# State products in four bands of PSUM rows, with a buffer of its own for the convolution gate, in a hybrid recurrent trunk on one core

## The chip, the cores and the metric

The kernel runs on one core of a Trainium2 chip. The metric is the device time of one execution in microseconds; the kernel before has a median of 1597.33 us over three runs (1597.06 to 1597.72). Engine names are those of the profile: PE is the matrix engine (PEld its weight loads), DVE the vector engine, ACT the activation engine, POOL the general one, SP issues the DMAs.

## The reference

One step of a one-layer trunk over 1072 tokens: 16 meta tokens, 1024 prompt tokens, and 8 samples of 4 tokens each. All of them share the weights; each sample starts from its own saved states.

```python
x = rmsnorm(h, norm_w)
z = x @ w_in                      # gates, and the inputs of four branches, 512 wide each
# A: GLA, 4 heads, key width 64     S_t = diag(exp g_t) S_{t-1} + k_t^T v_t ;  o_t = q_t S_t
# B: HGRN2, 4 heads, key width 128  the same recurrence with k = 1 - f
# C: mLSTM, 4 heads                 stabilised matrix memory
# D: conv module                    GLU -> causal depthwise conv, width 31 -> LayerNorm -> swish
y_b = W_b(silu(zgate_b) * mixer_b)
h = h + (sum_b sigmoid(gate_b) * y_b) @ w_out ;  out = rmsnorm(h, final_norm)
```

The outputs are the two token groups without the meta tokens, and the new states of the prompt and of each sample.

## The kernel before

All values are float32. A projection splits its weights and its activations into a high and a low part and adds three products for each block of 128 input features: in `mm3` these are L185, L186 and L187, in `pair` L277, L278 and L279. One projection of 128 output columns takes 24 matmuls for each group of about 356 tokens. `split_w` makes the two weight parts: the high one on ACT (L138), the low one on POOL, or on DVE where `E=V` is given (L139).

The program runs in stages, and each engine takes its instructions in one fixed order. That order is made before the run by a scheduler that simulates the program; it may move an instruction ahead of others whose operands it thinks will come later. `tc.cur_priority` pushes work back in that choice: the 31-tap convolution adds 700 to it.

1. **Entry (to about 100 us).** The 1072 token rows are read in nine tiles h0 to h8, normalised, transposed (L174) in three groups of three tiles, and evacuated as `xh` (ACT, L178) and `xl` (DVE, L179). One raw gate weight is loaded behind the first three tiles and split on DVE. A few gates (`gate_direct`) and the small projections (`small`) follow; `combine_x` makes the operand sums of the next stage.
2. **Pairs (about 90 to 500 us).** `pair` computes two projections of 128 columns at once by a Strassen-like scheme: seven half-size products instead of eight, each over 4 feature blocks and two token slices (s = 0, 1) of 268 columns. Its PSUM tiles are `sa` (tag a, two buffers, one for each slice) and `sb`, `sc`, `sd` (tag r, five buffers). There are 19 pairs: four `conv_pair` and fifteen `pair_to`. Each `conv_pair` is followed by the 31-tap convolution on DVE (`conv_taps`: one L386 and 30 L388 over 1024 columns), which reads its tile `u`; `u` has one buffer, and the next `conv_pair` writes its sigmoid into it (L349, ACT, straight from `sa`) before it multiplies it there (L352, DVE).
3. **Recurrences (about 500 to 1290 us).** Four HGRN2 units, two GLA units and four mLSTM units, with projections between them (`filler` adds gates). A recurrent unit projects f, k, q and v; `vtok` transposes v into token rows (`tta`, three PSUM tiles from `acc_tile`, which has three buffers in all, then `v9p` from the same ones); `levels` builds the intra-chunk attention in halving levels (`lv`, L636, after which DVE scales q and k in place, L651 and L652, before the next level may read them); `linear_unit` forms the chunk states and the outputs (`op`).
   In `linear_unit` the last chunk holds 16 prompt tokens and the 32 sample tokens, 48 rows (`TAIL`). Each sample's rows meet another state, so nine products go into one PSUM region: for each of them `qblk` holds a stationary block, zero but for the columns of that sample (48 columns wide in HGRN2, 112 in GLA, where two heads lie at rows 0 and 64). The attention inside the chunk is added by L816 (once or twice 48 rows). GLA also has diagonal sums `dg` (L760): nine products with 128 stationary columns and two moving ones.
4. **Branches and output (about 1290 us to the end).** Four branch projections, the gated sum and the output projection.

Of the kernel before, what the change touches and what calls it, by code (L numbers as in the profile page):

```python
# [65 lines left out]
def trunk(ctx, tc, hx, w_in, w_sm, w_br, w_out, pk, wgk2, mlb, fnorm, s_gla, s_hg, s_c, s_n, s_m, s_cv,  # L66
# [82 lines left out]
    with tc.tile_pool(name="x0", bufs=9, side="right", reuse_waits="tile") as x0:  # L149
        hs = []  # L150
# [7 lines left out]
        for i0 in (0, 3, 6):  # L158
# [9 lines left out]
            if i0 == 0:  # L168
                raw0 = load_raw(w_in, OFF["gate"])
# [10 lines left out]
            if i0 == 0:  # L180
                w0 = split_w(raw0, E=V)
# [70 lines left out]
    def pair(c0, c1, c11, c12, c22, c21):  # L252
# [20 lines left out]
        def prod(w, o, x, s, out, start, stop):  # L273
            xa, xb = (t[:, :, s * HS:(s + 1) * HS] for t in xs[x])
# [19 lines left out]
        for s in range(2):  # L294
            prod(w1, KH, "a12", s, a[s], False, True)
            c11(s, a[s])
# [7 lines left out]
        for s in range(2):  # L304
            prod(w4, 0, "s4", s, c[s], False, True)
            V.tensor_tensor(h(p1, s), h(u2, s), c[s], ALU.add)
# [6 lines left out]
    def pair_to(sec, i, dst, func, times=False, base=0):  # L313
# [27 lines left out]
        pair(o, o + P, c11, rest(i + 1, False), rest(i + 1, True), rest(i, True))  # L341

    def conv_pair(i):
        u = gtl("u", [P, UW + NSEQ * 34])
        us = u[:, UW:].rearrange("p (s x) -> p s x", x=34)
        G.memset(u[:, 0:30], 0.0)

        def c11(s, ps):
            S.activation(u[:, 30 + s * HS:30 + (s + 1) * HS], ps, AF.Sigmoid)  # L349

        def c12(t):
            V.tensor_tensor(u[:, 30:30 + HT], t, u[:, 30:30 + HT], ALU.mult)  # L352
# [88 lines left out]
    gate_direct(0, w=w0)  # L441
    gate_direct(1)
# [73 lines left out]
    qblk2 = mx.tile([P, (NSEQ + 1) * WT], F32, name="qblk", tag="qblk")  # L516
    G.memset(qblk2, 0.0)
    qblkb = [qblk2[:, 0:480], qblk2[:, 480:960]]
    cnt = {"att": 0}
# [10 lines left out]
    def csz(c):  # L530
        return min(P, NT - c * P)
# [43 lines left out]
    def vtok(sec, i, ones_col=False):  # L575
# [12 lines left out]
        v9 = split3(x9, 1, "v9", 4, acc_tile("v9p"))  # L588
# [109 lines left out]
    def qblk_both(qv):  # L698

        for i in range(2):  # L700
            r = slice(64 * i, 64 * i + 64)
            c = WT + 64 * i + NM
            for s in range(NSEQ):
                e = c + s * (WT + NDEC)
                G.tensor_copy(qblk2[r, e:e + NDEC], qv[r, i, NP + s * NDEC:NP + (s + 1) * NDEC])
            G.tensor_copy(qblk2[r, 64 * i:64 * i + NM], qv[r, i, NPR:NP])
        return lambda s: qblk2[:, s * WT:(s + 1) * WT]
# [8 lines left out]
    def z_out(o, rstd, nw, gate, zi, mu=None):  # L716
# [4 lines left out]
        else:  # L721
# [15 lines left out]
    def rms(os, epss):  # L737
# [4 lines left out]
        for i, o in enumerate(os):  # L742
# [3 lines left out]
            S.activation(sq[:TAIL, 8], o[:TAIL, 8], AF.Square, accum_out=ms[:TAIL, 9 * i + 8:9 * i + 9])  # L746
# [7 lines left out]
    def linear_unit(uid, qv, nh, k, f, prod, vts, s0, epss, finish, pout, sout):  # L754
        rw = P // nh
        if nh == 2:
            ps = mmt("dg")
            for c in range(9):
                n = csz(c)
                T.matmul(ps[:n, 2 * c:2 * c + 2], prod[:, c * P:c * P + n], onesb, start=True, stop=True)  # L760
# [49 lines left out]
        qb = qblk_both(qv) if nh == 2 else qblk_for(qv[:, 0], uid % 2)  # L810
        w = WT if nh == 2 else TAIL
        for s in range(1, NSEQ + 2):
            s %= NSEQ + 1
            T.matmul(ps[:w], qb(s), s0[:, s - 1] if s else sall[:, 7], start=(s == 1), stop=False)
# [532 lines left out]
```

## Time and profile before

| what | value |
|---|---|
| median of three runs | 1597.33 us |
| profiled execution, its own time | 1597.18 us |
| span of its trace | 1595.4 us |
| mean granted PE clock | 0.989 |
| DMA | 176.40 MB, mean 111 GB/s |
| DVE, ACT, POOL busy | 65%, 35%, 30% of the span |

The span leaves out 1.8 us of the execution's time. Averages say little here, since the four stages have different limits; the views of a window show each of them by itself. "Idle before, releaser" means how long an engine stood still before an instruction, and whose end let it go on. A matmul of float32 that is not a transpose or one of the split products shows as two instructions in the trace, since the array passes over it twice.

### The profile page before, as it was taken

What the parts mean: (1) busy time and instruction counts of PE and PEld (TensorE: products, weight loads), DVE (VectorE), ACT (ScalarE), POOL (GpSimd) and SP (SyncE); (2) the same over time, 40 slices, a digit from 0 to 9 for tenths busy, and PEclk for the clock granted to TensorE, in tenths of its full rate; (3) what the DMA queues carried; (4) which work ended last, traced back from release to release, by engine and by line L of the source; (5) the groups of instructions that cost most, each with busy time, mean ns of one, the idle gap of its engine ahead of it and who ended that gap; (6) DMA issues with size and microseconds to landing.
All of it is one profiled execution on the core that took longest, in us unless ns stands there. A gap on an engine that the chain in (4) does not pass through costs nothing.

```text
span 1595.4 us, 30033 instructions
## 1 busy us (share of the span) xinstructions
PE 1558.2 (98%) x12366; PEld 1496.5 (94%) x12366; DVE 1035.6 (65%) x1827; ACT 554.0 (35%) x1095; POOL 470.9 (30%) x418
## 2 busy tenths in 40 slices
PE   7999999899999999999999999999999999999998
PEld 6999999899999899999998998999999999999886
DVE  7959979999996446444544565476665646744533
ACT  6534343243433333323424323323323244422211
POOL 2222322123223232223232323222322313877300
PEclk9999999999999999999999999999999999999999
DMA  5423233231337113131323132144323277676231
GB/s 190 133 80 101 92 91 107 88 108 51 110 100 236 42 48 104 56 100 56 104 60 94 55 97 82 49 148 135 117 72 88 89 248 224 179 236 208 80 111 54
DMA packets 190572, 176.40 MB, mean 111 GB/s; under 512 B 9260, under 2 KB 164800, under 8 KB 190436
## 3 DMA queue, kind: packets, MB, share of 16 engines
q1 hardware_dynamic: 190436, 174.49, 35.6%
q8 instruction: 97, 1.59, 0.4%
q14 instruction: 39, 0.32, 0.1%
HBM read 122.45 MB, written 52.00 MB: 109 GB/s over the span
## 4 chain that ended last, share of the span: by engine, by line
PE 78%; DVE 16%; issue 3%; DMA 2%; ACT 1%; SPq 0%; DVEq 0%; POOLq 0%; ACTq 0%
PE acc L187 18%; PE acc L185 18%; PE acc L186 18%; DVE y L388 7%; PE lv L636 2%; DVE wl L139 2%; PE sa L277 1%; PE sa L278 1%; PE sa L279 1%; PE sc L278 1%; PE sc L277 1%; PE sc L279 1%; PE sd L279 1%; PE op L800 1%; PE sd L278 1%
## 5 line engine op out<-in xcount | busy, mean ns | idle before, releaser
L139 POOL TENSOR_TENSOR wl<-wraw,wh 128x1024 fp32r<-128x1024 f32 (+1 forms) x124 | 272.2, 2196 | 632.7 <-ACT wh L138 628.0
L185 PE MATMUL acc<-xh,wh 128*128 128x352 f32 (+2 forms) x1320 | 437.5, 332 | 2.1 <-ACT vt L539 1.2
L187 PE MATMUL acc<-xh,wl 128*128 128x352 f32 (+2 forms) x1320 | 436.7, 331 | 0.0
L186 PE MATMUL acc<-xl,wh 128*128 128x352 f32 (+2 forms) x1320 | 435.5, 330 | 0.0
L185 PEld LDWEIGHTS acc<-xh,wh 128*128 128x128 f32 x1320 | 251.7, 191 | 5.6 <-ACT vt L539 1.9
L187 PEld LDWEIGHTS acc<-xh,wl 128*128 128x128 f32 x1320 | 251.0, 190 | 3.2 <-issue 0.9
L186 PEld LDWEIGHTS acc<-xl,wh 128*128 128x128 f32 x1320 | 251.4, 190 | 1.8 <-issue 0.7
L388 DVE SCALAR_TENSOR_TENSOR y<-u,pkt,y 128x1024 f32<-128x1024 f32 x120 | 191.2, 1593 | 0.7
L138 ACT ACTIVATE wh<-wraw 128x512 fp32r<-128x512 f32 (+1 forms) x125 | 110.4, 883 | 231.0 <-PE acc L186 135.8
L185 PE MATMUL acc<-zh,wh 128*128 128x352 f32 x384 | 124.5, 324 | 0.0
L186 PE MATMUL acc<-zl,wh 128*128 128x352 f32 x384 | 124.3, 324 | 0.0
L187 PE MATMUL acc<-zh,wl 128*128 128x352 f32 x384 | 124.2, 324 | 0.0
L277 PE MATMUL sa<-xh,wh 128*128 128x268 f32 x304 | 88.7, 292 | 6.6 <-ACT u L349 6.3
L278 PE MATMUL sa<-xl,wh 128*128 128x268 f32 x304 | 88.2, 290 | 0.0
L279 PE MATMUL sa<-xh,wl 128*128 128x268 f32 x304 | 87.8, 290 | 0.0
L651 DVE TENSOR_TENSOR q<-q,tot 128x256 f32<-128x256 f32 (+3 forms) x96 | 46.4, 483 | 54.5 <-PE lv L636 53.7
L1179 POOL TENSOR_TENSOR mix<-mix,gt 128x352 f32<-128x352 f32 x72 | 73.1, 1030 | 28.9 <-DVE gt L1178 25.7
L185 PEld LDWEIGHTS acc<-zh,wh 128*128 128x128 f32 x384 | 72.2, 188 | 0.4 <-DVE gt L1178 0.4
L187 PEld LDWEIGHTS acc<-zh,wl 128*128 128x128 f32 x384 | 72.3, 188 | 0.0
L186 PEld LDWEIGHTS acc<-zl,wh 128*128 128x128 f32 x384 | 72.2, 188 | 0.0
L277 PEld LDWEIGHTS sa<-xh,wh 128*128 128x128 f32 x304 | 58.3, 192 | 7.3 <-ACT u L349 6.8
L1178 DVE TENSOR_TENSOR gt<-acc,gt 128x352 f32<-128x352 f32 x72 | 36.2, 518 | 39.5 <-PE acc L187 36.6
(393 smaller groups left out, 3367.3 us busy)
## 6 DMA issues: line engine op xcount, KB each, us to landing
wraw<-w_in SPq DMA_DIRECT2D x92, 512.0 KB, 3.9
gt<-gscr SPq DMA_DIRECT2D x30, 528.0 KB, 4.7
gscr<-gd SPq DMA_DIRECT2D x60, 176.0 KB, 1.8
zr<-zscr SPq DMA_DIRECT2D x16, 528.0 KB
wraw<-w_br SPq DMA_DIRECT2D x32, 256.0 KB, 2.9
gt<-sscr SPq DMA_DIRECT2D x12, 528.0 KB, 4.1
zscr<-gt SPq DMA_DIRECT2D x12, 528.0 KB, 2.6
sscr<-u SPq DMA_DIRECT2D x16, 268.0 KB, 2.3
```

The lines of the kernel that those rows point to most:

```text
L138: S.activation(hi[:, :kd], raw[:, :kd], AF.Copy)
L139: (E or G).tensor_tensor(lo[:, :kd], raw[:, :kd], hi[:, :kd], ALU.subtract)
L185: T.matmul(ps, wh(k), ah(k), start=(i == 0), stop=False)
L186: T.matmul(ps, wh(k), al(k), start=False, stop=False)
L187: T.matmul(ps, wl(k), ah(k), start=False, stop=(i == kd - 1))
L277: T.matmul(out, wh, xa[:, k], start=start and k == 0, stop=False, skip_group_check=True)
L278: T.matmul(out, wh, xb[:, k], start=False, stop=False, skip_group_check=True)
L279: T.matmul(out, wl, xa[:, k], start=False, stop=stop and k == KH - 1, skip_group_check=True)
L388: V.scalar_tensor_tensor(ymain, u[:, NM + j:NM + j + NPR], w(j), ymain, ALU.mult, ALU.add)
L651: V.tensor_tensor(qx[:, :, 1], qx[:, :, 1], pv[r, :, 0:1].broadcast_to([rw, nb, h]), ALU.mult)
L1178: V.tensor_tensor(gt[:, t0:t0 + n], ps[:, :n], gt[:, t0:t0 + n], ALU.mult)
L1179: G.tensor_tensor(mixed[j][:, t0:t0 + n], mixed[j][:, t0:t0 + n], gt[:, t0:t0 + n], ALU.add)
```

## The change

Seven edits, all in one kernel:

- **Last chunk in bands.** The 48 rows of the last chunk are spread over 128 PSUM rows. Two samples share a band of 32 rows, so a state product has 32 stationary columns (`qblk_bands`) and goes into one of four bands, in the order of samples 0, 2, 4, 6, 1, 3, 5, 7, then the prompt state (once for each head in GLA). The attention block is spread the same way into a new tile `attp` (48 x 128) by two ACT copies in HGRN2 and by two DVE operations for each head in GLA; these also take over the diagonal term, which a POOL multiply did before. The outputs, their mean squares and the last transposes then run over 128 rows, and `z_out` gathers the 48 columns again with two DVE operations in place of one.
- **Diagonal sums in bands.** Each of the nine `dg` products becomes up to four of 32 stationary columns, 34 for a GLA unit.
- **Fewer copies for `qblk`.** In GLA 6 POOL copies instead of 18, in HGRN2 3 instead of 2.
- **Convolution gate.** `conv_pair` writes its sigmoid into a tile of the tag `g11` (two buffers) instead of `u`.
- **Meta tokens.** In the fifteen `pair_to`, the products a12 and s4 leave out the 16 meta columns in the first slice: 252 columns instead of 268.
- **Entry.** Two gate weights are loaded behind the first three token tiles, and both are split on DVE, in the middle of the first group's transposes, instead of one there and one on POOL.
- **PSUM and tiles.** `v9p` takes a buffer of `mmt` instead of `acc_tile`; two small tiles share the buffer of another tag.

```diff
...
             if i0 == 0:
-                raw0 = load_raw(w_in, OFF["gate"])
+                raws = [load_raw(w_in, OFF["gate"] + j * P) for j in range(2)]
             for k in range(KD):
...
+                if i0 == 0 and k in (1, 5):
+                    wg01.append(split_w(raws[k // 4], E=V))
...
-        def prod(w, o, x, s, out, start, stop):
-            xa, xb = (t[:, :, s * HS:(s + 1) * HS] for t in xs[x])
+        def prod(w, o, x, s, out, start, stop, m=0):
+            m = m if s == 0 else 0
+            out = out[:, m:]
+            xa, xb = (t[:, :, s * HS + m:(s + 1) * HS] for t in xs[x])
...
-            prod(w1, KH, "a12", s, a[s], False, True)
+            prod(w1, KH, "a12", s, a[s], False, True, m)
...
         def c11(s, ps):
-            S.activation(u[:, 30 + s * HS:30 + (s + 1) * HS], ps, AF.Sigmoid)
+            S.activation(g11[:, s * HS:(s + 1) * HS], ps, AF.Sigmoid)
 
         def c12(t):
-            V.tensor_tensor(u[:, 30:30 + HT], t, u[:, 30:30 + HT], ALU.mult)
+            V.tensor_tensor(u[:, 30:30 + HT], t, g11, ALU.mult)
...
-        v9 = split3(x9, 1, "v9", 4, acc_tile("v9p"))
+        v9 = split3(x9, 1, "v9", 4, mmt("v9p"))
...
+    def spread(t, i):
+        return (t[:, 32 * i:32 * i + 32].rearrange("p (c x) -> p c x", x=16)[:, :, 8:16],
+                t.rearrange("p (s x) -> p s x", x=16)[:, :, 4 * i:4 * i + NDEC])
+
+    def dense(t):
+        return t[:, 0:NM].rearrange("p (c x) -> p c x", x=8), t[:, NM:TAIL].rearrange("p (s j) -> p s j", j=NDEC)
+
+    def qblk_bands(qv, nh, buf):
+        qb = qblk2[:, buf * 320:buf * 320 + 320]
+        for i in range(nh):
+            r = slice(i * (P // nh), (i + 1) * (P // nh))
+            q = qv[r, i, NPR:NT]
+            d = qb[r, 0:256].rearrange("p (b w) -> p b w", w=64)
+            sm = q[:, NM:].rearrange("p (b a j) -> p a b j", a=2, j=NDEC)
+            for a in range(2):
+                e = 48 * a + 4 * i
+                G.tensor_copy(d[:, :, e:e + NDEC], sm[:, a])
+            G.tensor_copy(spread(qb[r, 256:320], i)[0], dense(q)[0])
+        return lambda s: qb[:, 32 * s:32 * s + 32]
...
-                T.matmul(ps[:n, 2 * c:2 * c + 2], prod[:, c * P:c * P + n], onesb, start=True, stop=True)
+                for b in range(0, n, 32):
+                    e = min(b + 32, n)
+                    T.matmul(ps[b:e, 2 * c:2 * c + 2], prod[:, c * P + b:c * P + e], onesb, start=True, stop=True,
+                             skip_group_check=True)
...
-        w = WT if nh == 2 else TAIL
-        for s in range(1, NSEQ + 2):
-            s %= NSEQ + 1
-            T.matmul(ps[:w], qb(s), s0[:, s - 1] if s else sall[:, 7], start=(s == 1), stop=False)
+        for a in (0, 2, 4, 6, 1, 3, 5, 7, 8, 9)[:NSEQ + nh]:
+            b = 32 * (a // 2 if a < NSEQ else a - NSEQ)
+            T.matmul(ps[b:b + 32], qb(a), s0[:, a] if a < NSEQ else sall[:, 7], start=(a in (0, 2, 4, 6)), stop=False,
+                     skip_group_check=True)
         for hi_, ((vt, _), (_, att8)) in enumerate(zip(vts, atts)):
-            T.matmul(ps[64 * hi_:64 * hi_ + TAIL], att8, vt[:TAIL, 8, 0:P], start=False, stop=True)
+            for d, x, e in zip(spread(attp[hi_], hi_), dense(att8), dense(ident[:TAIL, :TAIL])):
+                if nh == 2:
+                    V.scalar_tensor_tensor(d, e, dgv[:TAIL, 8, hi_:hi_ + 1], x, ALU.mult, ALU.add)
+                else:
+                    S.activation(d, x, AF.Copy)
+            T.matmul(ps, attp[hi_], vt[:TAIL, 8, 0:P], start=False, stop=(hi_ == nh - 1), skip_group_check=True)
+        for o in outs:
+            S.activation(o[:, 8], ps, AF.Copy)
```

How the order moves on PE, at three places. A number behind a name tells tiles of one name apart; it differs by a few between the two kernels. The first place is the pair that follows the third `conv_pair`. Before, its `sb` came straight after the last products of the `conv_pair` (`sd_3012`):

```order
L279 MATMUL sd_3012<-xh_96,wl_2890 128x268
L277 MATMUL sd_3012<-xh_96,wh_2889 128x268
L278 MATMUL sd_3012<-xl_97,wh_2889 128x268
L279 MATMUL sd_3012<-xh_96,wl_2890 128x268
L277 MATMUL sb_3126<-sh_824,wh_3109 128x268
L278 MATMUL sb_3126<-sl_825,wh_3109 128x268
```

and its first `sa` some hundred matmuls later, behind its own `sc` and `sd`:

```order
L277 MATMUL sd_3239<-xh_96,wh_3116 128x268
L278 MATMUL sd_3239<-xl_97,wh_3116 128x268
L279 MATMUL sd_3239<-xh_96,wl_3117 128x268
L277 MATMUL sa_3124<-xh_96,wh_3102 128x268
L278 MATMUL sa_3124<-xl_97,wh_3102 128x268
L279 MATMUL sa_3124<-xh_96,wl_3103 128x268
```

In the changed kernel `sa` stands at the same place as in the program, ahead of `sb`:

```order
L282 MATMUL sd_3015<-xh_96,wl_2893 128x268
L280 MATMUL sd_3015<-xh_96,wh_2892 128x268
L281 MATMUL sd_3015<-xl_97,wh_2892 128x268
L282 MATMUL sd_3015<-xh_96,wl_2893 128x268
L280 MATMUL sa_3127<-xh_96,wh_3105 128x268
L281 MATMUL sa_3127<-xl_97,wh_3105 128x268
L282 MATMUL sa_3127<-xh_96,wl_3106 128x268
```

So `sa` moved ahead by about a hundred matmuls, and nothing but the two `sa` buffers of the `conv_pair` stands between them. The second place is the first GLA unit on PE, at the end of its second `vtok`. Before, the levels' products (`lv`) stood between the transposes (`tta`), and the next level followed at once:

```order
L538 MATMUL tta_9501<-ident_70,vf_9412 128x128 x2
L636 MATMUL lv_9595<-q_9114,k_9125 32x32 x3
L538 MATMUL tta_9501<-ident_70,vf_9412 128x128 x2
L538 MATMUL tta_9507<-ident_70,vf_9412 128x128
L636 MATMUL lv_9595<-q_9114,k_9125 32x32 x29
L640 MATMUL lvt_9631<-q_9114,k_9125 48x48
L538 MATMUL tta_9507<-ident_70,vf_9412 128x128 x3
L538 MATMUL tta_9513<-ident_70,vf_9412 48x128
L557 MATMUL v9p_9516<-ident_70,x9_9414 96x128
L636 MATMUL lv_9640<-q_9114,k_9125 32x32 x16
```

In the changed kernel the transposes stand together, the diagonal sums come behind them, and a projection follows:

```order
L547 MATMUL tta_9525<-ident_70,vf_9436 128x128 x4
L547 MATMUL tta_9531<-ident_70,vf_9436 128x128 x4
L547 MATMUL tta_9537<-ident_70,vf_9436 48x128
L566 MATMUL v9p_9540<-ident_70,x9_9438 96x128
L788 MATMUL dg_9551<-onesb_77,prod_9234 32x2 x33
L788 MATMUL dg_9551<-onesb_77,prod_9234 16x2
L649 MATMUL lvt_9635<-q_9138,k_9149 48x48
L185 MATMUL acc_9886<-xh_96,wh_9882 128x352
L186 MATMUL acc_9886<-xl_97,wh_9882 128x352
```

There each later level of this unit has 24 projection matmuls between itself and the level before it. The third place is the last chunk of the first HGRN2 unit, on PE; before:

```order
L802 MATMUL op<-sall,q 128x128
L814 MATMUL op<-s_5922,qblk 48x128 x8
L814 MATMUL op<-sall,qblk 48x128
L816 MATMUL op<-vt,att_5617 48x128
L187 MATMUL acc<-xh,wl 128x356
```

and in the changed kernel:

```order
L830 MATMUL op<-sall,q 128x128
L841 MATMUL op<-s_5930,qblk 32x128 x8
L841 MATMUL op<-sall,qblk 32x128
L849 MATMUL op<-vt,attp_5625 128x128
L186 MATMUL acc<-xl,wh 128x356
```

The neighbours are the same; the nine state products write 32 rows each, and the one that closes them writes all 128.

More of the change, by code (lines that the diff above doesn't have):

```diff
@@ L149, in trunk @@
     with tc.tile_pool(name="x0", bufs=9, side="right", reuse_waits="tile") as x0:
-        hs = []
+        hs, wg01 = [], []
         def load_h(i):
@@ L250, in combine_x, with pair @@
                   s3=(sh[:, 1], sl[:, 1]), s4=(sh[:, 2], sl[:, 2]))
-    def pair(c0, c1, c11, c12, c22, c21):
+    def pair(c0, c1, c11, c12, c22, c21, m=0):
         wp = pools["gph"]
@@ L304, in pair @@
         for s in range(2):
-            prod(w4, 0, "s4", s, c[s], False, True)
+            prod(w4, 0, "s4", s, c[s], False, True, m)
             V.tensor_tensor(h(p1, s), h(u2, s), c[s], ALU.add)
@@ L339, in rest @@
             return ev
-        pair(o, o + P, c11, rest(i + 1, False), rest(i + 1, True), rest(i, True))
+        pair(o, o + P, c11, rest(i + 1, False), rest(i + 1, True), rest(i, True), NM)
     def conv_pair(i):
         u = gtl("u", [P, UW + NSEQ * 34])
+        g11 = stt("g11")
         us = u[:, UW:].rearrange("p (s x) -> p s x", x=34)
@@ L440, in trunk @@
     open_pool("gph", bufs=1)
-    gate_direct(0, w=w0)
-    gate_direct(1)
+    for j in range(2):
+        gate_direct(j, w=wg01[j])
     small()
@@ L515, in trunk @@
     WT = 64 + TAIL
-    qblk2 = mx.tile([P, (NSEQ + 1) * WT], F32, name="qblk", tag="qblk")
+    qblk2 = mx.tile([P, 960], F32, name="qblk", tag="qblk")
     G.memset(qblk2, 0.0)
     qblkb = [qblk2[:, 0:480], qblk2[:, 480:960]]
+    attp = []
+    for i in range(2):
+        t = mx.tile([TAIL, P], F32, name=f"attp{i}", tag=f"attp{i}")
+        G.memset(t, 0.0)
+        attp.append(t)
     cnt = {"att": 0}
@@ L696, in qblk_for @@
         return lambda s: qb[:, s * TAIL:(s + 1) * TAIL]
[L698 to L707, printed above, removed]
+    def spread(t, i):
[15 more added lines that the diff above has]
+        return lambda s: qb[:, 32 * s:32 * s + 32]
     def vblk_for(v9, s0, s1):
@@ L714, in vblk_for, with z_out @@
         return vb
-    def z_out(o, rstd, nw, gate, zi, mu=None):
+    def z_out(o, rstd, nw, gate, zi, mu=None, head=0):
         if mu is not None:
@@ L724, in z_out @@
                                 ALU.mult)
-            V.tensor_scalar(o[:TAIL, 8], o[:TAIL, 8], rstd[:TAIL, 8:9], None, ALU.mult)
+            V.tensor_scalar(o[:, 8], o[:, 8], rstd[:, 8:9], None, ALU.mult)
         for c0, c1 in QUADS:
-            n = csz(c0)
+            bands = c0 == 8 and mu is None
+            n = P if bands else csz(c0)
             ps = mmt("zt")
@@ L730, in z_out @@
                 T.transpose(ps[:, (c - c0) * P:(c - c0) * P + n], o[:n, c, :], ident[:n, :n])
+            if bands:
+                for x, g in zip(spread(ps[:, :P], head), dense(gate[:, NPR - NM:])):
+                    V.scalar_tensor_tensor(g, x, nw, g, ALU.mult, ALU.mult)
+                continue
             a = NM if c0 == 0 else 0
@@ L964, in ml_n0 @@
     def ml_n0():
-        r = tl("n0", [32, P], 1)
+        r = tl("gd", [P, 352], 1, name="n0")[:32, :P]
         DMA.dma_start(r, s_n.rearrange("b h k -> (b h) k"))
@@ L1087, in ml_nout @@
         T.transpose(ps[:36, :P], nT, ident)
-        r = tl("n0", [36, P], 1, name="nout")
+        r = tl("gd", [P, 352], 1, name="nout")[:36, :P]
         V.tensor_copy(r, ps[:36, :P])
```

15 lines of the change are left out of this document (3 added, 12 removed).

## Prediction

> **What bounds the kernel now.** I read the page's busy line first, then the windows by stage, then the list of PE's waits, then the timeline where a wait or a low clock stood.
>
> ```profile
> PE 1558.2 (98%) x12366; PEld 1496.5 (94%) x12366; DVE 1035.6 (65%) x1827; ACT 554.0 (35%) x1095; POOL 470.9 (30%) x418
> ```
>
> PE stands still for 1595.4 - 1558.2 = 37 us in all, so the time is PE's work plus 37 us, and plus what the work loses to a low clock. The windows (span, then busy time of PE, PEld, DVE, ACT, POOL, then the granted PE clock, DMA share, GB/s) show where:
>
> ```profile
> 0.00:20.00 20.00, 11.47 (x53) 9.70 (x54) 11.46 (x30) 15.15 (x28) 6.03 (x20) 1.00 0.93 306
> ...
> 850.00:900.00 50.00, 47.70 (x606) 44.61 (x605) 30.75 (x66) 22.42 (x42) 16.40 (x28) 0.93 0.20 56
> 960.00:1000.00 40.00, 36.95 (x482) 34.24 (x481) 22.29 (x63) 14.41 (x32) 14.51 (x25) 0.91 0.25 72
> 1000.00:1290.00 290.00, 289.51 (x1939) 281.49 (x1938) 178.47 (x448) 89.88 (x206) 82.74 (x79) 1.00 0.35 107
> 1290.00:1595.40 305.40, 298.07 (x1686) 275.61 (x1684) 155.71 (x245) 96.44 (x189) 126.89 (x121) 0.99 0.52 164
> ```
>
> From 1000 us on PE is full at full clock but for the last few microseconds. So what PE saves earlier moves the end one for one, unless the saving meets another engine first. The one place where another engine is nearly as full is the pair stage (rows below): DVE works 82.49 of the 83.70 us of one convolution. PE's own waits (total, times, longest) are:
>
> ```profile
> PE xt L174 <- DVE ss L165: 8.1, 2, 7.9
> PE sa L277 <- ACT u L349: 6.3, 2, 4.8
> PE lv L636 <- DVE k L652: 4.8, 3, 1.9
> PE tta L538 <- ACT vf L581: 2.3, 1, 2.3
> PE acc L185 <- ACT vt L539: 1.2, 4, 0.3
> ```
>
> The change touches all five. A low clock is the second loss, at the windows cut where it changes:
>
> ```profile
> 294.13:298.97 4.84, 0.01 (x2) 0.01 (x1) 4.70 (x3) 0.45 (x2) 2.08 (x2) 0.79 0.00 0
> 297.00:303.80 6.80, 4.83 (x21) 4.83 (x22) 4.19 (x9) 1.34 (x4) 0.84 (x2) 0.50 0.52 157
> 549.60:553.00 3.40, 3.40 (x14) 3.40 (x13) 1.18 (x5) 0.46 (x1) 0.00 (x0) 0.50 0.14 53
> 856.80:860.20 3.40, 3.40 (x59) 2.96 (x60) 2.35 (x3) 0.91 (x3) 2.63 (x4) 0.50 0.60 154
> 877.20:880.70 3.50, 3.50 (x15) 3.50 (x14) 3.44 (x6) 0.96 (x1) 3.50 (x7) 0.51 0.58 152
> 966.00:969.40 3.40, 3.40 (x14) 2.85 (x15) 2.29 (x4) 2.31 (x4) 3.24 (x5) 0.50 0.60 156
> 979.60:983.10 3.50, 3.50 (x44) 3.46 (x45) 3.15 (x12) 0.00 (x0) 2.94 (x13) 0.51 0.04 12
> ```
>
> PE stood still for 4.84 us, and its clock was halved from 297.0 to 303.8 us. Of those 6.8 us PE worked 4.83, in which it does the work of 2.4: a loss of 2.4 us. A stretch of 3.4 us in which it works throughout loses 1.7 us.
>
> **The pairs.** The wait at 294 us reads thus:
>
> ```profile
> 298.52 0.68 ACT L349 ACTIVATE u<-sa 128x268 f32<-128x268 f32 x2 [5.02 <-DVE y L388]
> 298.97 0.59 PE L277 MATMUL sa<-xh,wh 128*128 128x268 f32 x1 [4.83 <-ACT u L349]
> ```
>
> ACT's sigmoid may not write `u` until the taps have read it; it holds both `sa` buffers, and PE the next pair. With a tile of its own it waits for nothing but its product. That takes away 6.3 us of waiting and the 2.4 us of low clock. The shorter products: each `pair_to` has 2 x 12 of them, 15 x 24 = 360, each 16 columns less. The price of a column is the slope between two pitches:
>
> ```profile
> 293.23 0.28 PE L277 MATMUL sd<-xh,wh 128*128 128x268 f32 x1
> 293.84 0.29 PE L279 MATMUL sd<-xh,wl 128*128 128x268 f32 x1
> ...
> 538.57 0.32 PE L186 MATMUL acc<-xl,wh 128*128 128x352 f32 x1
> 541.62 0.32 PE L187 MATMUL acc<-xh,wl 128*128 128x352 f32 x1
> ```
>
> The first two are five steps apart, 0.122 us each; the other two 19 steps, 0.1605 us each. The slope is 0.0385/84 = 0.46 ns a column, so 360 x 16 x 0.46 ns = 2.6 us. If PE sets the pace, the stage ends 6.3 + 2.4 + 2.6 = 11.3 us sooner.
>
> What is late next is DVE, whose work in this stage is not reduced: the taps stay, and c12 multiplies as before.
>
> ```profile
> 225.80:298.50 72.70, 67.35 (x537) 66.33 (x535) 72.30 (x72) 24.01 (x42) 17.19 (x7) 0.99 0.27 78
> 298.50:307.60 9.10, 8.63 (x52) 8.62 (x53) 6.24 (x14) 2.59 (x8) 0.84 (x2) 0.71 0.45 132
> 307.60:391.30 83.70, 82.81 (x666) 82.29 (x665) 82.49 (x96) 30.04 (x56) 19.37 (x9) 1.00 0.30 92
> 391.30:483.10 91.80, 91.52 (x740) 91.30 (x739) 91.77 (x109) 33.61 (x66) 27.36 (x10) 1.00 0.34 103
> ```
>
> From the second convolution's first tap to the last tap of the fourth (225.8 to 483.1 us) DVE idles 0.4 + 2.9 + 1.2 + 0 = 4.5 us. The second convolution can begin 2 us sooner (the first `sa` wait, 6.3 - 4.8 = 1.5, and about 0.5 of shorter products). So if DVE is saturated throughout, the last tap ends 6.5 us sooner. PE may run ahead of it by some of the 17.3 us of pairs that lay behind that tap, since the change lets the next pair begin under the taps. I take **-9**, between 6.5 and 11.3; the ends are -5 (DVE keeps an idle stretch) and -13.
>
> **State products in bands.** On PE the last chunk now reads:
>
> ```profile
> 586.13 1.96 PE L814 MATMUL op<-s,qblk 128*48 128x128 f32 x16
> 587.92 0.38 PE L814 MATMUL op<-sall,qblk 128*48 128x128 f32 x2
> 588.58 0.43 PE L187 MATMUL acc<-xh,wl 128*128 128x356 f32 x1
> ...
> 925.21 1.92 PE L814 MATMUL op<-s,qblk 128*112 128x128 f32 x16
> 927.62 0.43 PE L186 MATMUL acc<-xl,wh 128*128 128x352 f32 x1
> ```
>
> HGRN2 takes 588.58 - 586.13 = 2.45 us, GLA 2.41 us; a pass costs 1.79/16 = 0.112 us. Whether products in different bands run beside each other is to be seen in `lv`, which already writes bands of 32 rows:
>
> ```profile
> 541.87 0.77 PE L636 MATMUL lv<-q,k 128*32 128x32 f32 x64
> 542.57 0.29 PE L640 MATMUL lvt<-q,k 128*48 128x48 f32 x2
> ...
> 891.86 0.92 PE L636 MATMUL lv<-q,k 128*32 128x32 f32 x48
> 892.70 0.43 PE L185 MATMUL acc<-xh,wh 128*128 128x358 f32 x1
> ...
> L636 PE MATMUL lv<-q,k x48: 196/196/237, 891.9 to 892.6; 128*32 128x32 f32 x32, 128*32 128x64 f32 x16
> ```
>
> 64 passes took 0.70 us, 11 ns each, against 112 ns for a pass over all rows. The 48 at 891.86, 16 of them 64 columns wide, took 0.84 us. They do run side by side, at least the short ones. I take it that four bands overlap fully; then the longest band counts: three products (two samples and the prompt state), six passes, 0.67 us. HGRN2 adds the closing product over 128 rows, 0.22, and two changes between bands and whole rows, which I put at 0.15 each (the step into `lv` from 541.62 to 541.87 took 0.25 us instead of 0.16): 1.2 us, a gain of 1.25. GLA has two closing products: 1.4 us, a gain of 1.0 to 1.1. Four and two of these: **-7.2**. The ends are 0 (no overlap: 18 passes stay 18) and -9 (changes free).
>
> The copies into `attp`, the wider ACT evacuation and the extra DVE gather run beside projections and fillers (PE is full for 289.51 of 290 us while ACT works 90 and DVE 178). Without that cover the copies stand between the last level and the closing product, two ACT copies of the size of L349 or less, some 0.7 us a unit. I count nothing; the changed `qblk` copies lie on POOL, which works 83 of 290 us.
>
> **Diagonal sums.**
>
> ```profile
> 853.91 2.02 PE L760 MATMUL dg<-onesb,prod 128*128 128x2 f32 x18
> 855.86 0.33 PE L636 MATMUL lv<-q,k 128*32 128x32 f32 x14
> ```
>
> 18 passes take 1.95 us: loading 128 columns of weights sets the pace, not the two moving ones. In bands 34 products are 68 passes; at 11 ns that is 0.75 us, a gain of 1.2 for each of two units: **-2.4**, ends 0 and -3.
>
> One rule speaks against both edits. The Trainium skill, "TensorE: Matmul & The Clock Gate", Part 1, has a floor: "Start-to-start never drops below ≈25 ns however small N is". By it the 68 passes would take 1.7 us and this term would be -0.5. The time would be 1572, inside the forecast, so the rule has no chance of its own. The 11 ns of `lv` contradict it for products in different bands, and the sum keeps the trace's price.
>
> **GLA's waits.** `tta` waits 2.3 us, `lv` 4.8 us in three pieces, of which 1.9 us fall in the first HGRN2 unit (ahead of the low clock at 549.6) and 2.9 in the second GLA unit. In GLA that is 5.2 us, and four stretches at half clock lose 6.8. In the new order the transposes stand together ahead of the levels, and in the first unit each level has 24 projection matmuls (24 x 0.1605 = 3.9 us) between itself and the last, longer than the waits of 1.5 us. I take three quarters of the waits and half of the low clock: **-7**, ends -1 (moved elsewhere) and -12. For the first HGRN2 unit, whose order keeps its shape, I take **-1**, ends +1 and -3.6.
>
> **Small terms.** `v9p` in another pool frees the projection's accumulator sooner: 4 waits, 1.2 us, **-1.2**, ends 0 and -1.2. At the entry one load of 512 KB moves ahead of six token tiles; at 306 GB/s that is 1.7 us of delay, met by a DVE split that spares POOL's: **+0.5**, ends -1 and +2.5.
>
> **The sum.** -9 - 7.2 - 2.4 - 7 - 1 - 1.2 + 0.5 = -27.3. The profiled execution took 1597.18 us (its span of 1595.4 and 1.8 us around it), 0.15 below the median of the runs: 1597.2 - 27.3 = 1570 us.
>
> **Rivals.**
> - *DVE takes over in the pair stage.* For it: DVE's 4.5 idle us in 257. Against: PE can run ahead by part of a round. The term falls to -5 or -6.5, the time to 1573 to 1575. Chance 0.2.
> - *Bands do not overlap over 128 columns.* For it: the trace has no four-band product that long. Against: `lv` at 11 ns, and the 64-column passes at 891.86, which took no longer than (0.84 - 32 x 0.011)/16 = 0.03 us each. Both terms go: 1570 + 9.6 = 1580. Chance 0.1.
> - *GLA's waits move.* The DVE work of a level is the same, so a wait may stand before another level, with its half clock: 1570 + 7 = 1577. Chance 0.15.
> - *Slower: the closing product waits.* `attp` puts two copies between the last level and PE. If ACT or DVE comes to it late, PE, which takes instructions in order, stands still with a projection queued behind. A stall like that at 294 us costs 4.8 + 2.4 = 7.2 us; six units give +43, and from the fourth on (27.3/7.2 = 3.8) the kernel is slower: 1570 + 43 = 1613 at worst. Against: the levels end several microseconds ahead of `op`. Chance 0.03.
> - *The change does not do what it says*: the sigmoid still waits, now for `g11`, because `gate` pairs use the same two buffers; with the rest given back at the entry, 1590 to 1600. Chance 0.05, more than half of it still faster.
>
> The forecast itself, 1563 to 1573, has 0.43, and 0.04 is left for less than 1560. Each case has its own spread of a few microseconds. Leaving out the slower rival, the failed change and the outer tails, the range is 1560 to 1584. This kernel's measurement can tell about 0.2% (3 us) from no change. Faster 0.94, same 0.03, slower 0.03.
>
> **What would show it.** `sa <- ACT` should be gone from PE's waits; if PE then waits for DVE's `p`, `u` or `g` in the pairs, the first rival holds. The `op` products should take 1.2 to 1.4 us, `dg` 0.75. The windows 850 to 900 and 960 to 1000, earlier by what came before, should show a clock near 1. Wrong in all: a half clock over the pair stage, or PE waiting before each closing product.

## The result and the profile after

The changed kernel takes 1577.5 us (median of four runs, 1574.7 to 1578.83) against 1597.53 us before: 20 us less, a ratio of 0.9865 with a 95% interval of 0.984 to 0.9889. The forecast was 1570 with a range of 1560 to 1584, so the time lies inside the range and 7.5 us above the forecast itself. The profiled execution was the fastest of the four, 1574.7 us with a span of 1572.8 us. The trace shows 22.6 us less span; the other three runs took 2.8 to 4.1 us more than the profiled one.

The busy line of the page after:

```profile
PE 1536.2 (98%) x12470; PEld 1475.6 (94%) x12470; DVE 1040.9 (66%) x1840; ACT 555.8 (35%) x1108; POOL 464.8 (30%) x395
```

PE works 22.0 us less and still idles 36.6 us, as much as before. So the gain is work that became shorter, or was done at a higher clock, and the waits that went were replaced by others. The list of PE's waits after says which:

```profile
PE xt L174 <- DVE ss L165: 8.3, 3, 7.7
PE lv L645 <- DVE k L661: 6.6, 6, 1.4
PE acc L185 <- ACT xh L178: 2.6, 2, 1.9
PE sb L280 <- DVE p L309: 1.7, 2, 1.0
...
PE sa L280 <- DVE g L326: 1.0, 2, 0.5
...
PE tta L547 <- ACT vf L590: 0.8, 1, 0.8
...
PE sa L280 <- ACT p L289: 0.7, 1, 0.7
...
PE sd L280 <- DVE u L292: 0.5, 1, 0.5
PE sc L280 <- DVE p L309: 0.4, 1, 0.4
PE sd L280 <- ACT u L303: 0.4, 1, 0.4
```

`sa <- ACT u` with its 6.3 us is gone; six groups of small waits in the pairs stand in its place, 4.7 us in sum, four of them (3.6 us) for DVE. `tta <- ACT vf` fell from 2.3 to 0.8 us. `lv <- DVE k` did not fall: it rose from 4.8 us in three pieces to 6.6 us in six.

The windows after, over the pairs (from the first `sa` to the last `sd`), over the GLA units (from the last chunk of the fourth HGRN2 unit to that of the second GLA unit), and over the one stretch at half clock between the entry and the end:

```profile
90.86:492.92 402.06, 397.26 (x3214) 394.90 (x3212) 375.37 (x448) 145.43 (x282) 102.51 (x46) 1.00 0.34 100
...
806.04:1005.27 199.23, 190.86 (x2076) 181.06 (x2075) 114.29 (x253) 66.38 (x136) 55.90 (x50) 0.99 0.26 75
...
867.40:870.80 3.40, 3.40 (x13) 3.40 (x13) 3.31 (x10) 3.36 (x4) 0.11 (x1) 0.50 0.17 58
```

The same two stretches before, for comparison:

```profile
89.96:500.35 410.39, 401.89 (x3214) 399.88 (x3212) 373.87 (x448) 148.77 (x282) 101.21 (x46) 0.99 0.34 101
822.10:1025.20 203.10, 197.75 (x1945) 187.19 (x1944) 107.90 (x244) 62.55 (x131) 59.86 (x78) 0.97 0.24 72
```

The second number is the length, the third PE's busy time, the third from the end the granted clock. The pairs are 8.3 us shorter. In the GLA stretch PE's idle time grew from 5.35 to 8.37 us, although its clock rose from 0.97 to 0.99. The last chunks and the diagonal sums, on the timeline of PE after:

```profile
576.79 0.65 PE L841 MATMUL op<-s,qblk 128*32 128x128 f32 x16
577.25 0.38 PE L841 MATMUL op<-sall,qblk 128*32 128x128 f32 x2
577.56 0.48 PE L849 MATMUL op<-vt,attp 48*128 48x128 f32 x2
577.98 0.43 PE L186 MATMUL acc<-xl,wh 128*128 128x356 f32 x1
...
851.59 0.73 PE L788 MATMUL dg<-onesb,prod 128*32 128x2 f32 x68
852.25 0.29 PE L649 MATMUL lvt<-q,k 128*48 128x48 f32 x2
...
910.28 0.65 PE L841 MATMUL op<-s,qblk 128*32 128x128 f32 x16
910.74 0.39 PE L841 MATMUL op<-sall,qblk 128*32 128x128 f32 x4
911.06 0.71 PE L849 MATMUL op<-vt,attp 48*128 48x128 f32 x4
911.70 0.43 PE L185 MATMUL acc<-xh,wh 128*128 128x358 f32 x1
```

From the first state product to the next work it is 1.19 us in HGRN2 (2.45 before), 1.42 in GLA (2.41 before). The 68 passes of `dg` take 0.66 us (1.95 before), 10 ns each. The 16 passes of the samples start within 0.46 us (576.79 to 577.25): four bands at a time, 0.115 us each.

The sum of the forecast beside the trace, term by term:

| term | forecast | in the two traces |
|---|---|---|
| pairs | -9 | -8.3 (410.39 to 402.06) |
| state products | -7.2 | -6.8 (all `op` on PE, 41.7 to 34.9) |
| GLA's waits and clock | -7 | waits +3.0 (5.35 to 8.37), clock -5.1 at most: about -2.1 |
| diagonal sums | -2.4 | -2.65 (3.97 to 1.32) |
| first HGRN2 unit | -1 | -3.6 (its 1.9 us wait, and 1.7 of half clock at 549.6) |
| `v9p` | -1.2 | -0.6 (four waits of 0.3 became four of 0.15, for `tta`) |
| entry | +0.5 | +0.9 (first `sa` at 90.86 instead of 89.96) |
| not in the sum: transposes of `z_out` | 0 | -2.6 (12.66 to 10.10) |
| sum | -27.3 | -25.8, and -22.6 in span |

For `op`, `dg` and `zt` each pass counts from its start to the next start on PE, at most to its own end. The clock term takes four stretches of 3.4 us before against one after, 1.7 us each. Of the 3.2 us by which the list exceeds the span, 1.6 are new waits behind the second GLA unit (between PE's instructions 0.57 us before, 2.19 after); the rest is not allotted.

Two of the four stretches before, at 856.8 and 966.0 us, begin within 1.0 us of the end of a `dg`, and PE stood still for only 0.00 and 0.10 us in the 3.4 us ahead of them. The same two, with 0.00 to 0.11 us of idle time, are in the traces of two kernels below that keep this `dg` (the last transposes alone, and the kernel before with the low parts on DVE); a third one that keeps it (the gate's buffer alone) has none there. In the eight traces with `dg` in bands every stretch at half clock in GLA follows at least 1.8 us of idle time. So part of the clock term may belong to the diagonal sums and not to the order of the levels; no run separates the two.

### The profile page after: what moved, and what is told of

It is laid out like the page before. It is cut to its first block, busy times and chain, and to the rows that moved or that the text cites. A ratio compares the mean times of both kernels' runs of the same rounds, so it can differ in the third digit from the quotient of the medians.

```text
span 1572.8 us, 30258 instructions
## 1 busy us (share of the span) xinstructions
PE 1536.2 (98%) x12470; PEld 1475.6 (94%) x12470; DVE 1040.9 (66%) x1840; ACT 555.8 (35%) x1108; POOL 464.8 (30%) x395
## 4 chain that ended last, share of the span: by engine, by line
PE 74%; DVE 17%; issue 3%; DMA 2%; ACT 2%; POOL 0%; DVEq 0%; POOLq 0%; ACTq 0%; SPq 0%
PE acc L185 16%; PE acc L186 16%; PE acc L187 16%; DVE y L392 4%; PE lv L645 2%; DVE so L581 2%; DVE vt L581 2%; PE sa L280 1%; PE sa L281 1%; PE sa L282 1%; PE sc L280 1%; PE sc L281 1%; PE sc L282 1%; PE sd L281 1%; PE sd L280 1%
## 5 line engine op out<-in xcount | busy, mean ns | idle before, releaser
L139 POOL TENSOR_TENSOR wl<-wraw,wh 128x512 fp32r<-128x512 f32 (+1 forms) x123 | 279.2, 2272 | 632.0 <-ACT wh L138 569.4
L392 DVE SCALAR_TENSOR_TENSOR y<-u,pkt,y 128x1024 f32<-128x1024 f32 x120 | 193.8, 1615 | 0.6
L280 PE MATMUL sa<-xh,wh 128*128 128x268 f32 (+1 forms) x304 | 87.4, 288 | 1.7 <-DVE g L326 1.0
L281 PE MATMUL sa<-xl,wh 128*128 128x268 f32 (+1 forms) x304 | 86.6, 285 | 0.0
L282 PE MATMUL sa<-xh,wl 128*128 128x268 f32 (+1 forms) x304 | 86.6, 285 | 0.0
```

Of the source, the lines that this page charges most:

```text
L139: (E or G).tensor_tensor(lo[:, :kd], raw[:, :kd], hi[:, :kd], ALU.subtract)
L280: T.matmul(out, wh, xa[:, k], start=start and k == 0, stop=False, skip_group_check=True)
L281: T.matmul(out, wh, xb[:, k], start=False, stop=False, skip_group_check=True)
L282: T.matmul(out, wl, xa[:, k], start=False, stop=stop and k == KH - 1, skip_group_check=True)
L392: V.scalar_tensor_tensor(ymain, u[:, NM + j:NM + j + NPR], w(j), ymain, ALU.mult, ALU.add)
```

## The experiments

Seven kernels undo or add one edit, one changes an order, one repeats the changed kernel, and one puts three edits together. "Before" in the expectations is the kernel before; each result gives the times on its own chip.

**The changed kernel again**, for the spread of its runs.

> The changed kernel once more, to see how far its own runs lie apart. If the differences between its four runs (1574.7 to 1578.8) come from stretches at half clock that fall differently each time, the times again spread over 3 to 4 us and the profile with the higher time shows one or two more such stretches of 3.4 us (1.7 us each); if the spread came from one disturbed run, they agree within 1 us.

Measured: 1576.5 us (1575.49 to 1577.16) against 1595.87; ratio 0.9882, interval 0.9859 to 0.9904. The spread was 1.7 us, between the two expectations, and the runs' clocks (0.995 to 0.997) do not follow their times. The cause of the earlier spread stays open. The gain of 19 to 20 us is confirmed, and with it that differences of less than 2 us between kernels need more than their times.

**The gate's buffer alone**, on the kernel before:

```diff
+        g11 = stt("g11")
...
-            S.activation(u[:, 30 + s * HS:30 + (s + 1) * HS], ps, AF.Sigmoid)
+            S.activation(g11[:, s * HS:(s + 1) * HS], ps, AF.Sigmoid)
...
-            V.tensor_tensor(u[:, 30:30 + HT], t, u[:, 30:30 + HT], ALU.mult)
+            V.tensor_tensor(u[:, 30:30 + HT], t, g11, ALU.mult)
```

> The kernel before with one edit: the convolution gate has its own buffer. Theory: the wait of sa for ACT's sigmoid (6.3 us) and its half clock (2.4 us) go, and DVE becomes the next limit, so PE gets 3 to 4 us of new waits for DVE; the pair stage ends 5 to 6 us sooner and the kernel takes 1591 to 1593. Rival: DVE was the limit all along and the wait only shows where it is felt; then the stage ends within 1.5 us of 500.35 and the kernel takes 1596 to 1597.5.

**And undone** in the changed kernel (the same lines backwards).

> The changed kernel with that one edit taken back. Theory: the same 5 to 6 us come back, 1582 to 1584, with sa waiting for ACT 5 us or more. Rival (DVE the limit all along): 1577 to 1579.

Measured: alone 1585.79 us against 1595.87 (ratio 0.9941, interval 0.9919 to 0.9964), 10 us less and more than expected; undone 1582.01 us, 5.5 us more than the changed kernel on the same chip. With the edit undone the old wait is back, with the same longest piece:

```profile
PE sa L280 <- ACT u L352: 6.3, 3, 4.8
```

What a reader should look at is the pair stage, since the edit reorders everything behind it:

| kernel | pairs, us | PE idle in them | POOL busy | DVE busy |
|---|---|---|---|---|
| before | 410.39 | 8.50 | 101.2 | 373.9 |
| gate's buffer alone | 403.66 | 3.47 | 104.7 | 375.2 |
| changed, gate undone | 407.89 | 9.37 | 91.7 | 374.5 |
| changed | 402.06 | 4.80 | 102.5 | 375.4 |
| changed, low parts on DVE | 394.23 | 0.00 | 8.8 | 354.1 |
| before, low parts on DVE | 404.37 | 4.95 | 8.1 | 363.8 |

The buffer is worth 6.7 us there by the one comparison and 5.8 by the other; the other edits, the shorter products among them, 1.6 to 2.5. DVE was not the limit all along, but of the 3.5 and 4.8 us that PE still idles there with the buffer, 3.2 and 3.6 us are listed as waits for it. The rest of the first kernel's gain lies around the pairs: its first `sa` starts 1.3 us sooner, the half clock of the first HGRN2 unit (1.7 us) does not occur, and the GLA stretch is 1.0 us shorter, without any edit there. The 1.9 us wait of the first HGRN2 unit is still in it:

```profile
PE lv L637 <- DVE k L653: 1.9, 1, 1.9
```

It is absent in the changed kernel with the gate undone, so another edit took it away; in that order, as in the changed kernel's, 33 projection matmuls instead of 21 stand between the first level and the second. Which edit moved them was not tested.

**The pairs' low weight parts on DVE instead of POOL**, in the changed kernel:

```diff
-        w1 = split_w(r0)
+        w1 = split_w(r0, E=V)
...
-        w4 = split_w(r1[:, KH:], KH)
+        w4 = split_w(r1[:, KH:], KH, E=V)
```

> The changed kernel with the low weight parts of every pair (w1 and w4) made on DVE instead of POOL. Theory: in the pairs DVE is now the limit, and what makes it slow is POOL: a tap takes 1.27 us alone and up to 3.4 us beside POOL's subtraction (mean 1.62). On DVE the two parts cost 1.2 and 0.6 us a pair, the taps come down to 1.3 us, PE's waits for DVE in the pairs (about 5 us) halve, and the kernel takes 1574 to 1576. Rival: DVE has simply too much to do; 1.8 us more for each pair makes PE wait 10 us or more longer, 1585 or above.

Measured: 1571.92 us, 4.6 less than the changed kernel on the same chip (ratio to before 0.9854, interval 0.9833 to 0.9876). The groups of the 30 taps, after the change and then with this edit (count x, then busy us, mean ns):

```profile
L392 DVE SCALAR_TENSOR_TENSOR y<-u,pkt,y 128x1024 f32<-128x1024 f32 x120 | 193.8, 1615 | 0.6
```

```profile
L392 DVE SCALAR_TENSOR_TENSOR y<-u,pkt,y 128x1024 f32<-128x1024 f32 x120 | 155.0, 1292 | 0.2
```

and the windows 225 to 480 us, after and then with this edit:

```profile
225.00:480.00 255.00, 250.20 (x2016) 247.85 (x2015) 251.87 (x292) 89.14 (x176) 66.85 (x28) 1.00 0.33 97
```

```profile
225.00:480.00 255.00, 255.00 (x2080) 254.95 (x2080) 237.79 (x316) 98.69 (x182) 4.98 (x5) 1.00 0.35 106
```

DVE was given more work (316 instructions instead of 292 in the same 255 us) and was busy 14 us less, PE stood still for nothing, and the pairs took 7.8 us less, 4.8 of it idle time. The kernel gained less than its pairs, since the GLA stretch took 201.8 us instead of 199.2 and the HGRN2 units before it 1.3 us more. The taps lost 38.8 us. So DVE was the limit in the changed kernel, and what made it so was POOL beside it. Which operations suffer shows in the groups by line in the changed kernel (ns minimum, median, maximum); the tap has two large operands in SBUF, `p<-u,sc` reads one of two from PSUM:

```profile
L309 DVE TENSOR_TENSOR p<-u,sc x38: 418/421/434, 107.8 to 490.2; 128x268 f32<-128x268 f32 x38
...
L304 DVE TENSOR_TENSOR u<-u,p x19: 701/707/1806, 106.4 to 487.7; 128x536 f32<-128x536 f32 x19
...
L392 DVE SCALAR_TENSOR_TENSOR y<-u,pkt,y x120: 1268/1276/3429, 123.0 to 485.1; 128x1024 f32<-128x1024 f32 x120
```

The Trainium skill, "GPSIMD Engine Reference", Specifications, says that POOL shares its SBUF interfaces with DVE, with contention for DVE instructions that have two SBUF inputs or run in a two-port mode. The rows agree: the one with a PSUM operand never takes over 434 ns in 38 times, the other two up to 2.6 and 2.7 times their median. The agreement is thin for the first, because only two of the 38 overlap a POOL subtraction by more than 0.1 us (418 and 422 ns; in the trace before, six, at 418 to 427). Of the 42 taps with such an overlap 26 stretch, and 16 keep 1.27 to 1.29 us.

**The same edit on the kernel before.**

> The kernel before with the pairs' low weight parts on DVE and nothing else. Theory: the taps that hold u are slow because POOL's subtraction runs beside them, so without it they end before the next convolution's sigmoid is due; the wait of sa for ACT (6.3 us, and 2.4 us of half clock) goes away without a buffer, and the kernel takes 1585 to 1590. Rival: the wait depends on the place of the taps in DVE's order, not on their speed; the wait stays at 4 us or more and the time at 1592 or above.

Measured: 1588.14 us against 1595.59 (ratio 0.9956, interval 0.9939 to 0.9972). Neither account holds alone. The time is that of the first, but the wait is still there:

```profile
PE sa L277 <- ACT u L349: 5.0, 1, 5.0
```

The last three taps ahead of that sigmoid run at full speed:

```profile
290.15 3.92 DVE L388 SCALAR_TENSOR_TENSOR y<-u,pkt,y 128x1024 f32<-128x1024 f32 x3
```

They still end at 294.07, and ACT's sigmoid starts at 294.17. So the place of the taps in DVE's order keeps this wait whole; what fell is the other of the two waits and the small ones (pairs 410.39 to 404.37, 3.5 us of it idle time; the other 2.5 lie in PE's busy time and are not allotted). Faster taps and a buffer of its own for the gate are two different gains.

**State products band by band**, in the changed kernel:

```diff
-        for a in (0, 2, 4, 6, 1, 3, 5, 7, 8, 9)[:NSEQ + nh]:
+        for a in ((0, 1, 8, 2, 3, 4, 5, 6, 7) if nh == 1 else (0, 1, 8, 2, 3, 9, 4, 5, 6, 7)):
```

> The changed kernel with the state products of a unit issued band by band (samples 0, 1 and the prompt state into the first band, then 2 and 3 into the second, and so on) instead of going round the four bands. The same products, the same rows. Theory: PE starts its products in order and only neighbours in different bands run side by side, so most of the overlap is lost; a last chunk that took 1.2 us (HGRN2) takes some 1.9 to 2.1, and the six of them cost 4 to 5 us: 1580 to 1582. Rival: each band has its own queue and the order does not matter: 1.2 us as before, 1575 to 1578.

Measured: 1575.92 us (ratio 0.9861), the same time; my theory fell. The timeline of the first unit:

```profile
577.62 0.68 PE L841 MATMUL op<-s,qblk 128*32 128x128 f32 x10
578.08 0.27 PE L841 MATMUL op<-sall,qblk 128*32 128x128 f32 x1
578.11 0.30 PE L841 MATMUL op<-s,qblk 128*32 128x128 f32 x3
578.19 0.27 PE L841 MATMUL op<-sall,qblk 128*32 128x128 f32 x1
578.23 0.30 PE L841 MATMUL op<-s,qblk 128*32 128x128 f32 x3
578.45 0.48 PE L849 MATMUL op<-vt,attp 48*128 48x128 f32 x2
```

In the program's text `sall` is the third product, behind two samples. In the trace ten passes of the samples start ahead of its first pass at 578.08: later products, in other bands, overtook it. (The trace does not hold the order in which PE was given the products; that it is the order of the text is taken from the kernel.) All 18 passes took 0.83 us instead of 0.77 (576.79 to 577.56 in the fence above). In GLA the order costs more:

```profile
910.33 0.65 PE L841 MATMUL op<-s,qblk 128*32 128x128 f32 x6
...
911.40 0.71 PE L849 MATMUL op<-vt,attp 48*128 48x128 f32 x4
912.04 0.43 PE L185 MATMUL acc<-xh,wh 128*128 128x358 f32 x1
```

Its 20 passes took 1.07 us instead of 0.78, and the last chunk 1.71 instead of 1.42. So the bands overlap in either order, and the worse one costs 0.06 us a unit in HGRN2 and 0.29 in GLA, 0.8 us in all six.

**Only the last transposes**, on the kernel before:

```diff
             n = csz(c0)
+            m = P if mu is None else n
...
-                T.transpose(ps[:, (c - c0) * P:(c - c0) * P + n], o[:n, c, :], ident[:n, :n])
+                T.transpose(ps[:, (c - c0) * P:(c - c0) * P + m], o[:m, c, :], ident[:m, :m])
...
+            G.memset(o[:, 8], 0.0)
```

> The kernel before, but the last transposes of a unit (z_out, third part) read all 128 rows of a tile that is cleared first, instead of 48 rows. Nothing else; the 48 columns used afterwards are the same. In the changed kernel the transposes of z_out take 2.55 us less in sum, which the prediction did not have. Theory: a transpose of 48 rows is slow by itself or at the change of rows, so this edit alone brings 2 to 2.6 us of the zt time (12.66 to about 10.1) and a time of 1593 to 1595. Rival: the zt time fell with the new order around it; then it stays within 0.5 us of 12.66 here.

Measured: 1595.29 us over ten runs against 1597.86 (ratio 0.9983, interval 0.9971 to 0.9995). The `zt` passes fell from 12.66 to 11.20 us: 1.5 of the 2.6, between the two expectations. At six of the eight places a projection follows the last transpose; there the step into it, the transpose itself and the first projection matmul took 0.66 us with 48 rows and 0.38 with 128. So the change of rows costs 0.28 us a time. The remaining 1.1 us were not tested, and part of them is the count: in the changed kernel's order a projection matmul stands behind the first four transposes at three places instead of one, and takes over 0.08 us of theirs each time.

**The entry undone**, in the changed kernel:

```diff
-                raws = [load_raw(w_in, OFF["gate"] + j * P) for j in range(2)]
+                raw0 = load_raw(w_in, OFF["gate"])
...
-                if i0 == 0 and k in (1, 5):
-                    wg01.append(split_w(raws[k // 4], E=V))
+            if i0 == 0:
+                wg01.append(split_w(raw0, E=V))
...
-    for j in range(2):
-        gate_direct(j, w=wg01[j])
+    gate_direct(0, w=wg01[0])
+    gate_direct(1)
```

> The changed kernel with the entry of before: one gate weight behind the first three token tiles, the second one split on POOL. Theory: the second load delays the later token tiles; without it the first product of the pairs starts 0.9 us sooner (90.0 instead of 90.9 in the trace) and the kernel gains 0.5 to 1.5 us. Rival: the early weight pays for its delay, and the time is the same or up to 1.5 us longer.

Measured: 1574.59 us (1572.69 to 1576.45); ratio 0.9858, interval 0.9841 to 0.9874, against 0.9865 and 0.9882 for the changed kernel. That is 1 to 4 us less, with intervals that overlap, so the times alone do not settle it. In the trace the first `sa` starts at 89.2 us; in the six traces here that have the edit it starts at 90.0 to 92.4, and in the other five without it at 88.7 to 90.0. So the edit at the entry costs about 2 us by the traces, 1 to 3 us against this one; the sign was forecast, and the size lies toward the upper of its ends.

**GLA's diagonal term on ACT**, in the changed kernel:

```diff
-                G.tensor_tensor(o[:, 0:8], vt[:, 0:8, 0:P], dgv[:, 0:8, hi_:hi_ + 1].broadcast_to([P, 8, P]), ALU.mult)
+                for c in range(8):
+                    S.activation(o[:, c], vt[:, c, 0:P], AF.Identity, scale=dgv[:, c, hi_:hi_ + 1])
```

> The changed kernel with the diagonal term of GLA (the product of vt and dg over 8 chunks) made by eight ACT instructions a head instead of one POOL instruction of 1.9 to 2.1 us. Theory: in the first GLA unit DVE's scaling of q and k took 2.5 and 2.0 us beside that POOL instruction, against 0.9 and 0.45 without, and PE's waits for it (0.8 us at 858, and part of the later ones) follow from it; they fall, the GLA part (863 to 1005 us) gets 1 to 3 us shorter: 1573 to 1576. Rival: the waits come from the chain level by level and from DVE standing behind a DMA, not from POOL; then no gain, 1576 to 1579.

Measured: 1567.63 us (1566.81 to 1568.71) against 1597.86; ratio 0.9811, interval 0.9796 to 0.9825. That is 9 to 11 us less than the changed kernel by the ratios, three times the upper end of what was expected. In the first GLA unit before the change, POOL's product for one head lay beside one scaling of q, and the k behind it was short:

```profile
857.38 1.90 POOL L793 TENSOR_TENSOR o<-vt,dg 128x1024 f32<-128x1024 f32 x1 [0.39 <-ACT vt L539]
...
857.82 2.28 DVE L651 TENSOR_TENSOR q<-q,f 64x256 f32<-64x256 f32 x2 [1.62 <-PE lv L636]
860.12 0.43 DVE L652 TENSOR_TENSOR k<-k,f 128x256 f32<-128x256 f32 x1
```

DVE in the same unit after the change:

```profile
853.66 2.51 DVE L660 TENSOR_TENSOR q<-q,f 64x280 f32<-64x280 f32 x2
856.20 2.04 DVE L661 TENSOR_TENSOR k<-k,f 128x280 f32<-128x280 f32 x1
858.16 0.28 DVE L678 COPY_PREDICATED att<-lvmt,lvt 48x24 f32<-48x24 uint8 x2
862.28 1.28 DVE L930 SCALAR_TENSOR_TENSOR ab<-f 128x1072 f32<-128x1072 f32 x1 [3.84 <-DMA f<-fscr]
```

the POOL instructions beside it, now for both heads in a row:

```profile
853.76 4.18 POOL L822 TENSOR_TENSOR o<-vt,dg 128x1024 f32<-128x1024 f32 x2 [0.78 <-DVE dg L792]
```

and DVE with the term on ACT:

```profile
854.78 0.91 DVE L660 TENSOR_TENSOR q<-q,f 64x280 f32<-64x280 f32 x2
855.72 0.45 DVE L661 TENSOR_TENSOR k<-k,f 128x280 f32<-128x280 f32 x1
856.09 0.29 DVE L678 COPY_PREDICATED att<-lvmt,lvt 48x24 f32<-48x24 uint8 x2
859.76 1.27 DVE L931 SCALAR_TENSOR_TENSOR ab<-f 128x1072 f32<-128x1072 f32 x1 [3.39 <-DMA f<-fscr]
```

The scaling of q and k of this level took 4.6 us beside POOL and 1.4 us without, and the same in the second unit (948.7 us after the change). `f` has one buffer, so the load of the next unit's `f` can only start when that `k` is done (it is issued at 858.27 us, and at 856.20 with the term on ACT), and DVE, which takes instructions in order, waits for the load at L930 with the next level queued behind it. The GLA stretch with the term on ACT:

```profile
807.15:998.36 191.21, 188.77 (x2074) 179.17 (x2074) 108.45 (x253) 75.67 (x168) 48.09 (x46) 1.00 0.27 78
```

It is 8.0 us shorter than after the change (199.23); PE idles 2.44 us in it instead of 8.37, and no stretch at half clock is left between the entry and the end of the kernel.

**Three edits together** on the changed kernel: the low parts on DVE, the diagonal term on ACT, the entry of before.

> The changed kernel with three edits together: the pairs' low weight parts on DVE (4 to 5 us alone), GLA's diagonal term on ACT (9 us alone) and the entry of before (2 us alone). Theory: they act in different stretches (pairs, 850 to 1000 us, entry) and add up to 13 to 16 us on 1576.5: 1560 to 1564. Rival: the entry and the pairs feed the same DVE queue, and the clock's stretches at half speed fall anew, so that only the largest counts: 1566 to 1569.

Measured: 1560.9 us (1559.75 to 1561.69) against 1595.59; ratio 0.9784, interval 0.9762 to 0.9805. It beats both kernels, by 35 and by 13 to 16 us. The three gains add up, as expected, and the trace shows each: pairs of 394.2 us, a GLA stretch of 193.1 us, and the first `sa` at 89.1 us.

## Why the prediction was right, and where not

- **The bound.** Right: PE's work moves the end. Its busy time fell by 22.0 us and the span by 22.6.
- **Pairs, -9.** Right in size (-8.3) and in kind: the forecast put it between PE's limit and DVE's. The wait of `sa` for the sigmoid went, DVE's `p`, `g` and `u` came, as the first rival had it, at a smaller price than its own. What the step had not seen is why DVE is slow. It took the taps' mean as given; 39 us of it were POOL's doing.
- **State products, -7.2, and diagonal sums, -2.4.** Right: -6.8 and -2.65. Four bands do overlap fully over 128 columns (six passes in a row, 0.11 us apart, for all 18). HGRN2 gained 1.26 us a unit and GLA 1.0, as forecast. The rival without overlap is out, and the 25 ns floor of the Trainium skill ("TensorE: Matmul & The Clock Gate", Part 1) does not hold for products in different bands: `dg` took 0.66 us for 68 passes.
- **GLA, -7: this step failed.** The prediction said that with 24 projection matmuls (3.9 us) between levels the waits of 1.5 us would be covered, and took three quarters of them away. They grew, from 5.35 to 8.37 us. The mis-sized quantity is the DVE time of a level: the step took it as it stood before. With the transposes together and `dg` done sooner, POOL's two products came to lie beside q and k of the first level, which took 4.6 us, more than the 24 matmuls cover, instead of 1.4; the load of `f` came later, and the later levels with it. The run with that product on ACT shows it: waits 2.44 us, 8 us off the stretch. Not all of the growth need come from there: with the gate's buffer alone, where nothing in GLA is edited, the waits of this stretch are 7.06 us. The half clock fell by more than the step took (5.1 us at most, for 3.4), and part of that may be the work of `dg`, which the step did not consider. The third rival (the waits move elsewhere, +7 on the forecast: 1577) describes the result best.
- **First HGRN2 unit, -1.** Its wait and half clock went whole, -3.6, the end of its range. The half clock is no sure follower of this wait: the wait stands at 1.9 us in the trace before and in three others (the last transposes alone, the gate's buffer alone, the low parts on DVE alone), and half clock follows it in the first two and not in the last two. The wait went with another edit than the gate's, which no run singles out.
- **Entry, +0.5.** +0.9 in the trace, 1 to 3 by its undoing.
- **Transposes of `z_out`.** Left out of the sum: -2.6 as counted here, of which 1.5 are the 48-row shape.
- **The sum.** That -25.8 in the trace comes so near to -27.3 is partly luck: GLA brought 5 us less than was taken, and the first HGRN2 unit and the transposes together 5 us more.
- **The slower rival and the one without effect** are out: PE's list of waits has no `op` behind `attp` and no `sa` behind a sigmoid.

## What to carry to other kernels

Where an engine is named as the next limit, ask not only how long its instructions are but why some of them take two or three times as long as others of the same shape: a mean of 1615 ns over taps of 1276 ns median was worth more than most of the edits. Work on POOL that looks free, on an engine that is busy a third of the time, can be paid for by DVE; giving it to DVE or ACT may make DVE less busy. And when an edit lets something start sooner, look at what it will then run beside.

## What the runs showed of the hardware that was not expected

- DVE instructions with two SBUF operands stretch beside a POOL instruction with two: taps 1.27 us alone, up to 3.43 us beside it (26 of 42 that overlap one); a 128 x 280 product 0.45 us alone and 2.04 us beside it. A product with one PSUM operand stays at 0.42 us, in the few times that the two overlap.
- Products in different bands of 32 PSUM rows do not keep the program's order: issued band by band they overtook each other, and took 0.83 us instead of 0.77 for 18 passes and 1.07 instead of 0.78 for 20.
- A step between shapes costs PE about 0.1 us. The two closing passes of HGRN2 (48 rows of weights, 128 columns) took 0.42 us and the four of GLA 0.64: two passes more cost 0.11 us each, as a pass of the full shape does, and what the first and the last take beyond that lies at the change.
- Half clock can come without idle time: behind 18 passes of `dg` with two moving columns each (2 us), PE ran at half clock from 856.8 us although it had stood still for 0.00 us in the 3.4 us before. A wait of 1.9 us, on the other hand, was followed by half clock in two traces and not in two others.
